# Up projections of a two-layer trunk: when products and operand sums are rounded, and when a group is convolved

## The chip, the cores and the metric

The kernel runs on one NeuronCore of a Trainium2 chip. The metric is the device time of one execution in microseconds (us), the median of several runs. The engines of the core work side by side and each takes its instructions in the order in which the program holds them: TensorE (PE) multiplies matrices, VectorE (DVE) and ScalarE (ACT) work element by element, GpSimd (POOL) and SyncE (SP) mostly issue DMAs. An instruction that reads what another engine made waits for that engine.

## The reference, cut to what matters

A trunk of two layers on 256 tokens of width 2048: a gated linear attention and a block-sparse attention, each followed by a gated FFN with a short convolution. Only the FFN matters here.

```python
def conv_ffn(x, norm_w, w_up, conv_w, conv_b, w_down):
    S = x.shape[1]
    h = rms_norm(x, norm_w) @ w_up                    # 256 x 2048 times 2048 x 11264
    hp = jnp.pad(h, ((0, 0), (CONV_WIDTH - 1, 0), (0, 0)))
    acc = conv_b
    for j in range(CONV_WIDTH):                       # width 3
        acc = acc + conv_w[j] * hp[:, j:j + S]
    a, u = jnp.split(acc, 2, axis=-1)
    return (jax.nn.silu(a) * u) @ w_down              # hidden 5632
```

## The kernel before, in words

**Precision and pieces.** All products are made in float32 accuracy from two rounded parts of each operand: a high part (`hi`) and the rest (`lo`), with three products hi·hi, hi·lo and lo·hi. Weights stream from HBM through SP into `wraw` tiles of 128 x 2048 (a chunk) and are split in pieces of 128 x 1024 at most: ACT rounds a piece to `whi` (L155), DVE subtracts to get `wlo` (L157). PE reads both. `step()` hands out one piece after the other; a "piece" is the unit in which the kernel counts time, and `after(n, job)` puts a job n pieces later.

**Blocks of seven products.** The up projection has 22 groups (J = 0 to 21) of 512 columns. Most are plain (L323, L326). Five pairs, the blocks that begin at J = 0, 4, 8, 12 and 16, are done together with fewer products: for chosen k a chunk yields seven products instead of eight (a "seven"). For a seven DVE makes sums of the weights (`t13` and `t24`, L116 to L118), and its four pieces are b11, wide, t13 and t24; DVE also makes sums of the activations (`comb`, in `combine`: L341 to L344), which are split like all operands (L482 on ACT, L483 on DVE). The order of k in a block is written out by hand in `ORDERS`; a `+` there marks a seven.

**From a group to the hidden operand.** A group's result is scaled, transposed into `z`, stored to DRAM and loaded back turned (`upT`, four DMAs on POOL). After `lag_of(J)` pieces `convolve` makes the taps of its first half (ACT L866, DVE L871 and L873), two pieces later those of the second half, then the product with silu (`product`: ACT L877, DVE L878), then `hidden`, which splits it to `hid` (L482 on ACT, L483 on DVE). The down projection reads `hid`. For J in `EARLY` = (1, 3, 5, 7, 9, 11, 13) `hidden` also starts the activation sums of the down projection's sevens: `combine` makes `comb` on DVE at once, and `rounded` splits it some pieces later.

**What sets the order.** The program is written piece by piece as above; then a scheduler of the tile framework fixes the order of each engine's instructions from its own estimates before the program runs. So a job that is moved by a piece also changes the order of its neighbours, on PE too.

Of the kernel before, what the change touches and what calls it, by code (L numbers as in the profile page):

```python
# [173 lines left out]
def trunk(ctx: ExitStack, tc: tile.TileContext, xT, x0g, x_tok, cst, msk, w1p, w2a, w_k, w_qa, w_v2, w_v, w_gs, w_g, w_go,  # L174
# [14 lines left out]
    def slot(shape, dt, name):  # L189
        return big.tile(shape, dt, name=name, tag="slot")  # L190

    def temp(name, shape=(128, 2, S), dt=F32):
        return tmp.tile(list(shape), dt, name=name, tag="temp")
# [81 lines left out]
    def col(c):  # L275
        return gn[:, c - C_GN:c - C_GN + 1] if C_GN <= c < C_GN + KT else cs[:, c:c + 1]
# [25 lines left out]
    def after(steps, job):  # L302
        later.append((cur[0] + steps, job))
# [10 lines left out]
    def gemm_tok(xs, groups=1, evacuate=lambda ps: ps):  # L314
        out_ = [accs() for _ in range(groups)]
        for q0 in range(0, KT, 2):
            for ps in out_:
                hi, lo = step()
                for ks in ((0,), (1,)) if cur[0] < 3 and groups > 1 else ((0, 1),):
                    tiles_ = [(q0 + k, t, k * 512) for k in ks for t in range(2)]  # L320
                    for x0 in (0, S):
                        for kt, t, c in tiles_:
                            T.matmul(ps[t], xs(kt)[:, x0 + 128 * t:x0 + 128 * t + 128], hi[:, c:c + 512],  # L323
                                     start=kt == 0 and x0 == 0, stop=False)
                    for kt, t, c in tiles_:
                        mm = T.matmul(ps[t], xs(kt)[:, 128 * t:128 * t + 128], lo[:, c:c + 512],  # L326
                                      start=False, stop=kt == KT - 1)
                newest[:] = [mm.ins]
        got = out_ if groups > 1 else evacuate(out_[0])
        ws.prefetch(cur[0])  # L330
        return got

    def behind(job):
        with ws.behind():
            job()

    def combine(k, halves_, into, wait=0):

        (a0, a1), (b0, b1) = halves_
        t = temp("comb", (128, 4, 128))  # L340
        V.tensor_add(t[:, 0], a1, b1)  # L341
        V.tensor_sub(t[:, 1], t[:, 0], a0)
        V.tensor_sub(t[:, 2], a0, a1)
        V.tensor_sub(t[:, 3], b0, t[:, 1])  # L344

        def rounded():
            c = slot([128, 4, 2, 128], F32R, "comb")
            split(c[:, :, 0], c[:, :, 1], t)
            into[k] = c

        if wait:
            after(wait, lambda: behind(rounded))
        else:
            rounded()
# [6 lines left out]
    def combine_late(k, xs, into, far=False):  # L361
        behind(lambda: combine_parts(k, xs, into, 5 if far else 2))
# [115 lines left out]
    def rows(xs):  # L478
        return lambda kt: xs[kt // 2][:, kt % 2, :]

    def split(dst_hi, dst_lo, src):
        A.copy(dst_hi, src)  # L482
        V.tensor_sub(dst_lo, src, dst_hi.bitcast(F32))  # L483
# [343 lines left out]
    def lag_of(J):  # L827

        if J + 1 in BLOCKS:
            order, n_tail = ORDERS["up"][BLOCKS.index(J + 1)]  # L830
            pairs = sum(seven for _, seven in order)
            return 2 * len(order) + 2 * pairs if pairs > 1 else 2 * (len(order) - n_tail) + 2 * pairs + 2
        if J - 1 in BLOCKS:
            return 13
        return 9 if J < FT // 2 - 2 else 7

    def ffn(layer, nrm, then):
        xs = rows(nrm.xs)
        hid, sums = [], {}
        cw = C_CW + layer * 3 * 2 * FT  # L840
        cb = C_CB + layer * 2 * FT
        turned = dram.tile([FT // 2, 16, 32, 4, 64], F32, name=f"turned{layer}")

        def square(ps):
            z = slot([128, 16, 2, 32], F32, "z")
            for t in range(2):
                tok = temp("tok", (128, 512))
                A.activation(tok, ps[t], AF.Copy, scale=nrm.woven[:, t:t + 1])
                V.transpose(z[:, :, t, :], tok.rearrange("p (a b) -> p a b", b=32))
            return z  # L850

        def store(J, z):
            nc.gpsimd.dma_start(turned[J].rearrange("(a i) r q c -> (i r) a (q c)", a=4),  # L853
                              z.rearrange("p (a q) t c -> p a (q t c)", a=4))

        def load(J):
            f = slot([128, 4, S], F32, "upT")
            for q in range(4):
                nc.gpsimd.dma_start(f[32 * q:32 * q + 32].rearrange("p a (i c) -> p (a i) c", i=4),  # L859
                                  turned[J][:, :, q, :].rearrange("a r c -> r a c"))  # L860
            return f

        def taps(j, t, au):
            for i in range(2):
                n = i * FT + j
                A.activation(au[i][:, j % 2, :], t[:, i, :], AF.Identity, bias=col(cb + n),  # L866
                             scale=col(cw + 2 * 2 * FT + n))
            for i in range(2):
                n = i * FT + j
                u = au[i][:, j % 2]  # L870
                V.scalar_tensor_tensor(u[:, 1:], t[:, i, :S - 1], col(cw + 2 * FT + n), u[:, 1:],  # L871
                                       op0=OP.mult, op1=OP.add)
                V.scalar_tensor_tensor(u[:, 2:], t[:, i, :S - 2], col(cw + n), u[:, 2:],  # L873
                                       op0=OP.mult, op1=OP.add)

        def product(au):
            A.activation(au[0], au[0], AF.Silu)  # L877
            V.tensor_mul(au[0], au[0], au[1])  # L878

        def hidden(J, au):  # L880
            hid.append(slot([128, 2, 2 * S], F32R, "hid"))
            split(hid[-1][:, :, :S], hid[-1][:, :, S:], au[0])
            if J in EARLY:
                combine(J, [(au[0][:, i, :128], au[0][:, i, 128:]) for i in range(2)], sums, 1)

        def convolve(J, t):
            au = temp("gate"), temp("value")
            behind(lambda: taps(2 * J, t[:, 0:2, :], au))
            after(2, lambda: behind(lambda: taps(2 * J + 1, t[:, 2:4, :], au)))
            after(3, lambda: behind(lambda: product(au)))  # L890
            after(4, lambda: behind(lambda: hidden(J, au)))

        f, first = {}, {}

        def onto(J, z):
            lag = lag_of(J)
            after(1, lambda: store(J, z))
            after(max(lag - 7, 2), lambda: f.update({J: load(J)}))
            after(lag, lambda: convolve(J, f[J]))

        def up_rows(t, J, x):
            if t == 0:
                first[J] = slot([128, 16, 2, 32], F32, "z")
            A.activation(x, x, AF.Copy, scale=nrm.woven[:, t:t + 1])
            V.transpose(first[J][:, :, t, :], x.rearrange("p (a b) -> p a b", b=32))  # L905
            if t:
                onto(J, first[J])

        x_sums = {}
        for J in range(FT // 2):  # L910
            if J == 2:
                after(1, lambda: combine_late(6, nrm.xs, x_sums))
            if J in BLOCKS:
                b = BLOCKS.index(J)
                down("up", nrm.xs, x_sums, None, lambda t, c, x: up_rows(t, J + c - 2 * b, x), {}, b)
            elif J in GROUPS:
                onto(J, gemm_tok(xs, 1, square))
        then(hid, sums)
# [380 lines left out]
```

## Time and profile before

| | us |
|---|---|
| median of 3 runs | 2144.72 |
| lowest and highest run | 2143.65, 2145.70 |
| profiled execution | 2145.70 |
| its span (first to last instruction) | 2143.9 |
| PE busy | 2135.4 |
| DVE busy | 1858.5 |
| ACT busy | 1346.8 |
| POOL busy | 290.1 |

The first conv-FFN's up projections lie between about 380 and 843 us of the span, the second's between about 1447 and 1913. "Busy" of PE means that a matmul was under way; the clock granted to it was 1.00 throughout. A row of the timeline gives the start, the duration, the engine, the line and what it writes and reads; a bracket at its end tells how long the engine was idle before it and what ended that. Consecutive instructions on DVE and ACT overlap a little, so what an instruction costs its queue is the distance from its start to the next start.

### The profile page before, as it was taken

How to read it: one execution, taken by the hardware profiler on the slowest of the kernel's cores; microseconds unless marked ns; L12 is line 12 of the kernel's file. 1: busy time of each engine (PE TensorE's matmuls, PEld its weight loads, DVE VectorE, ACT ScalarE, POOL GpSimd, SP SyncE). 2: the span in 40 equal slices, each digit the busy share in tenths (PEclk: the TensorE clock that was granted, in tenths of full speed). 3: DMA queues.
4: the chain of work that ended last, by engine and by line, in shares of the span. 5: the costliest groups of instructions: out<-in, count | busy, mean ns of one | idle time of the engine just before them, and what ended most of it. 6: DMA issues, size and time to landing. Idle time of an engine off the chain costs nothing.

```text
span 2143.9 us, 27139 instructions
## 1 busy us (share of the span) xinstructions
PE 2135.4 (100%) x9565; PEld 1767.7 (82%) x9565; DVE 1858.5 (87%) x2548; ACT 1346.8 (63%) x1881; POOL 290.1 (14%) x448
## 2 busy tenths in 40 slices
PE   9999999999999999999999999999999999999999
PEld 7888888888888888888888888888888878888887
DVE  6887788889999988998888789988899899879987
ACT  6657666566666666656566776555666666656554
POOL 1011111011021111000022341011110111210000
PEclk9999999999999999999999999999999999999999
DMA  8566677577687787575667986666776877775655
GB/s 323 182 222 212 215 243 275 203 241 252 219 266 252 236 265 248 205 255 217 226 252 258 285 283 210 227 244 209 240 256 218 260 249 236 262 248 207 245 205 168
DMA packets 90170, 510.11 MB, mean 238 GB/s; under 512 B 13569, under 2 KB 14609, under 8 KB 40114
## 3 DMA queue, kind: packets, MB, share of 16 engines
q1 hardware_dynamic: 60434, 417.31, 54.3%
q0 software_dynamic: 29024, 90.28, 15.4%
q8 instruction: 75, 1.23, 0.2%
q10 hardware_dynamic: 576, 0.79, 0.1%
q14 instruction: 61, 0.50, 0.1%
HBM read 463.22 MB, written 45.11 MB: 237 GB/s over the span
## 4 chain that ended last, share of the span: by engine, by line
PE 98%; DVE 1%; DMA 1%; issue 0%; ACT 0%; SPq 0%; ACTq 0%; DVEq 0%
PE p L404 55%; PE acc L323 27%; PE acc L326 13%; DVE wlo L157 1%; PE hf L941 0%; DMA wraw<-w_up1s 0%; PE sT L752 0%; PE o L769 0%; DMA wraw<-w_v 0%; PE s L1054 0%; ACT whi L155 0%; PE z L607 0%; PE o L555 0%; PE s L1052 0%; DVE t L116 0%
## 5 line engine op out<-in xcount | busy, mean ns | idle before, releaser
L155 ACT CAST whi<-wraw 128x1024 fp32r<-128x1024 f32 (+1 forms) x786 | 773.5, 1003 | 436.5 <-PE acc L323 212.1
L157 DVE TENSOR_TENSOR wlo<-wraw,whi 128x1024 fp32r<-128x1024 f32 (+1 forms) x786 | 899.9, 1160 | 165.2 <-ACT whi L155 141.2
L323 PE MATMUL acc<-whi,xw 128*128 128x512 f32 x2176 | 540.2, 389 | 0.7 <-ACT whi L155 0.6
L323 PEld LDWEIGHTS acc<-whi,xw 128*128 128x128 f32 x2176 | 407.6, 188 | 86.6 <-ACT whi L155 2.2
L404 PE MATMUL p<-whi,xw 128*128 128x512 f32 x1294 | 344.1, 389 | 0.0
L326 PE MATMUL acc<-wlo,xw 128*128 128x512 f32 x1088 | 291.9, 389 | 0.0
L404 PEld LDWEIGHTS p<-whi,xw 128*128 128x128 f32 x1294 | 242.8, 188 | 50.3 <-ACT whi L155 0.2
L404 PE MATMUL p<-whi,hid 128*128 128x512 f32 x1038 | 281.1, 389 | 0.0
L155 ACT CAST whi<-t 128x1024 fp32r<-128x1024 f32 x168 | 174.0, 1052 | 142.1 <-PE p L404 94.2
L326 PEld LDWEIGHTS acc<-wlo,xw 128*128 128x128 f32 x1088 | 204.1, 188 | 42.6 <-DVE wlo L157 0.3
L404 PEld LDWEIGHTS p<-whi,hid 128*128 128x128 f32 x1038 | 194.7, 188 | 40.3
L157 DVE TENSOR_TENSOR wlo<-t,whi 128x1024 fp32r<-128x1024 f32 x168 | 202.3, 1221 | 23.9 <-ACT whi L155 17.4
L404 PE MATMUL p<-whi,comb 128*128 128x512 f32 x672 | 218.8, 390 | 2.1 <-ACT whi L155 2.1
L404 PE MATMUL p<-wlo,xw 128*128 128x512 f32 x647 | 185.6, 390 | 0.0
L859 POOL DMA_DIRECT2D upT<-turned x176 | 114.1, 655 | 311.0 <-DVE wlo L157 82.4
L404 PEld LDWEIGHTS p<-whi,comb 128*128 128x128 f32 x672 | 126.1, 188 | 29.8 <-ACT whi L155 3.8
L404 PE MATMUL p<-wlo,hid 128*128 128x512 f32 x519 | 150.6, 389 | 0.0
L404 PEld LDWEIGHTS p<-wlo,xw 128*128 128x128 f32 x647 | 121.5, 188 | 25.0
L404 PE MATMUL p<-wlo,comb 128*128 128x512 f32 x336 | 115.6, 389 | 0.0
L404 PEld LDWEIGHTS p<-wlo,hid 128*128 128x128 f32 x519 | 97.4, 188 | 20.3
L116 DVE TENSOR_TENSOR t<-wraw 128x1024 f32<-128x1024 f32 x84 | 102.5, 1220 | 13.4 <-DMA wraw<-w_dn 6.0
L853 POOL DMA_DIRECT2D turned<-z x44 | 34.1, 775 | 502.5 <-DVE z L905 189.3
(257 smaller groups left out, 2259.8 us busy)
## 6 DMA issues: line engine op xcount, KB each, us to landing
wraw<-w_up SPq DMA_DIRECT2D x96, 1024.0 KB, 5.5
wraw<-w_dn SPq DMA_DIRECT2D x88, 1024.0 KB, 4.9
wraw<-w_up0s SPq DMA_DIRECT2D x40, 1024.0 KB, 5.7
wraw<-w_up1s SPq DMA_DIRECT2D x40, 1024.0 KB, 5.4
turned<-z POOLq DMA_DIRECT2D x44, 512.0 KB, 4.7
upT<-turned POOLq DMA_DIRECT2D x176, 128.0 KB, 5.4
wraw<-w_go SPq DMA_DIRECT2D x16, 1024.0 KB, 5.7
wraw<-w_kk SPq DMA_DIRECT2D x16, 1024.0 KB, 6.3
```

The costliest lines, as they stand in the source:

```text
L116: V.tensor_sub(t13, src[:, 512:1536], src[:, 0:1024])
L155: one = nc.scalar.copy(hi[:, a:b], src[:, a:b])
L157: two = nc.vector.tensor_sub(lo[:, a:b], src[:, a:b], hi[:, a:b].bitcast(F32))
L323: T.matmul(ps[t], xs(kt)[:, x0 + 128 * t:x0 + 128 * t + 128], hi[:, c:c + 512], start=kt == 0 and x0 == 0, stop=False)
L326: mm = T.matmul(ps[t], xs(kt)[:, 128 * t:128 * t + 128], lo[:, c:c + 512], start=False, stop=kt == KT - 1)
L404: mm = T.matmul(p[n], x[xi], w[wi][:, 512 * f:512 * f + 512], start=n not in begun, stop=left[n] == 0)
L853: nc.gpsimd.dma_start(turned[J].rearrange("(a i) r q c -> (i r) a (q c)", a=4), z.rearrange("p (a q) t c -> p a (q t c)", a=4))
L859: nc.gpsimd.dma_start(f[32 * q:32 * q + 32].rearrange("p a (i c) -> p (a i) c", i=4), turned[J][:, :, q, :].rearrange("a r c -> r a c"))
```

## The change

Three numbers. A block's second group (J = 1, 5, 9, 13, 17) is convolved 14 pieces after its products instead of 13, which also loads its `upT` one piece later. Every group's product is split to `hid` five pieces after its convolution began instead of four. And the activation sums of the groups in `EARLY` are rounded three pieces after that instead of one.

```diff
@@ lag_of @@
         if J - 1 in BLOCKS:
-            return 13
+            return 14
@@ hidden @@
             if J in EARLY:
-                combine(J, [(au[0][:, i, :128], au[0][:, i, 128:]) for i in range(2)], sums, 1)
+                combine(J, [(au[0][:, i, :128], au[0][:, i, 128:]) for i in range(2)], sums, 3)
@@ convolve @@
             after(3, lambda: behind(lambda: product(au)))
-            after(4, lambda: behind(lambda: hidden(J, au)))
+            after(5, lambda: behind(lambda: hidden(J, au)))
```

The order moves on PE, DVE and ACT; on POOL and SP it is the same. Three places follow, all in layer 0; the other blocks and layer 1 show the same pattern. Names carry buffer numbers.

ACT in block 4, around the split of the first t24 piece, `whi_4173`. Before (`gate_4053` belongs to J = 2, `gate_3952` and `comb_4064` to J = 1):

```order
L482 CAST hid_4061<-gate_3952 128x2x256
L482 CAST comb_4091<-comb_4064 128x4x128
L155 CAST whi_4094<-wraw_3964 128x1024
L866 ACTIVATE gate_4053<-upT_3894,cs_82 128x256
L866 ACTIVATE value_4054<-upT_3894,cs_82 128x256
L155 CAST whi_4118<-wraw_3986 128x512
L155 CAST whi_4136<-wraw_3986 128x1024
L155 CAST whi_4157<-t13_4070 128x1024
L877 ACTIVATE gate_4053<-gate_4053 128x512
L482 CAST hid_4154<-gate_4053 128x2x256
L155 CAST whi_4173<-t24_4071 128x1024
L155 CAST whi_4186<-wraw_4033 128x1024
```

Now (`gate_4051` is J = 2, `gate_3974` and `comb_4104` J = 1):

```order
L877 ACTIVATE gate_3974<-gate_3974 128x512
L155 CAST whi_4083<-wraw_3956 128x1024
L866 ACTIVATE gate_4051<-upT_3894,cs_82 128x256
L866 ACTIVATE value_4052<-upT_3894,cs_82 128x256
L155 CAST whi_4115<-wraw_3986 128x512
L482 CAST hid_4101<-gate_3974 128x2x256
L155 CAST whi_4133<-wraw_3986 128x1024
L155 CAST whi_4151<-t13_4062 128x1024
L877 ACTIVATE gate_4051<-gate_4051 128x512
L482 CAST hid_4167<-gate_4051 128x2x256
L482 CAST comb_4170<-comb_4104 128x4x128
L155 CAST whi_4173<-t24_4063 128x1024
```

The rounding of `comb` stood four splits ahead of `whi_4173` and stands directly before it now, behind `hid`.

DVE in the same place. Before:

```order
L157 TENSOR_TENSOR wlo_4137<-wraw_3986,whi_4136 128x1024
L157 TENSOR_TENSOR wlo_4158<-t13_4070,whi_4157 128x1024
L878 TENSOR_TENSOR gate_4053<-gate_4053,value_4054 128x512
L483 TENSOR_TENSOR hid_4154<-gate_4053,hid_4154 128x2x256
L157 TENSOR_TENSOR wlo_4174<-t24_4071,whi_4173 128x1024
L116 TENSOR_TENSOR t13_4181<-wraw_4098 128x1024
```

Now:

```order
L342 TENSOR_TENSOR comb_4104<-comb_4104,gate_3974 128x128
L157 TENSOR_TENSOR wlo_4152<-t13_4062,whi_4151 128x1024
L344 TENSOR_TENSOR comb_4104<-gate_3974,comb_4104 128x128
L878 TENSOR_TENSOR gate_4051<-gate_4051,value_4052 128x512
L483 TENSOR_TENSOR hid_4167<-gate_4051,hid_4167 128x2x256
L483 TENSOR_TENSOR comb_4170<-comb_4104,comb_4170 128x4x128
L157 TENSOR_TENSOR wlo_4174<-t24_4063,whi_4173 128x1024
```

Two of the activation sums (L342, L344) now stand ahead of the product L878, and the rest of `comb` (L483) ahead of `wlo_4174`.

DVE before block 8, where J = 5's second half is convolved (`gate_4691` before, `gate_4713` now). Before:

```order
L157 TENSOR_TENSOR wlo_4722<-wraw_4611,whi_4721 128x1024
L871 SCALAR_TENSOR_TENSOR gate_4691<-upT_4534,cs_82,gate_4691 128x255
L871 SCALAR_TENSOR_TENSOR value_4692<-upT_4534,cs_82,value_4692 128x255
L873 SCALAR_TENSOR_TENSOR gate_4691<-upT_4534,cs_82,gate_4691 128x254
L873 SCALAR_TENSOR_TENSOR value_4692<-upT_4534,cs_82,value_4692 128x254
L157 TENSOR_TENSOR wlo_4746<-wraw_4658,whi_4745 128x1024
L849 STREAM_TRANSPOSE z_4761<-tok_4762 128x16x32
```

Now:

```order
L157 TENSOR_TENSOR wlo_4722<-wraw_4611,whi_4721 128x1024
L157 TENSOR_TENSOR wlo_4740<-wraw_4658,whi_4739 128x1024
L849 STREAM_TRANSPOSE z_4755<-tok_4756 128x16x32
L849 STREAM_TRANSPOSE z_4755<-tok_4759 128x16x32
L157 TENSOR_TENSOR wlo_4763<-wraw_4658,whi_4762 128x1024
L871 SCALAR_TENSOR_TENSOR gate_4713<-upT_4547,cs_82,gate_4713 128x255
L116 TENSOR_TENSOR t13_4801<-wraw_4725 128x1024
L871 SCALAR_TENSOR_TENSOR value_4714<-upT_4547,cs_82,value_4714 128x255
L871 SCALAR_TENSOR_TENSOR gate_4790<-upT_4625,cs_82,gate_4790 128x255
L873 SCALAR_TENSOR_TENSOR gate_4713<-upT_4547,cs_82,gate_4713 128x254
```

The four taps of that half moved from between two plain pieces to behind two more splits, among the block's own work.

PE at the end of block 8's sevens. Before:

```order
L404 MATMUL p6_4953<-whi_5043,comb_3740 128x512
L404 MATMUL p4_4778<-whi_5043,xw_3328 128x512
L404 MATMUL p3_4777<-wlo_5017,comb_3740 128x512
L404 MATMUL p2_4776<-wlo_5017,xw_3328 128x512
L404 MATMUL p2_4776<-whi_5050,xw_3338 128x512 x4
L404 MATMUL p5_4941<-wlo_5034,comb_3740 128x512
L404 MATMUL p7_4942<-wlo_5034,comb_3740 128x512
```

Now:

```order
L404 MATMUL p3_4775<-wlo_5017,comb_3740 128x512
L404 MATMUL p2_4774<-wlo_5017,xw_3328 128x512
L404 MATMUL p5_4941<-wlo_5034,comb_3740 128x512
L404 MATMUL p7_4942<-wlo_5034,comb_3740 128x512
L404 MATMUL p6_4953<-whi_5043,comb_3740 128x512
L404 MATMUL p4_4776<-whi_5043,xw_3328 128x512
L404 MATMUL p6_4953<-whi_5043,comb_3740 128x512
L404 MATMUL p4_4776<-whi_5043,xw_3328 128x512
L404 MATMUL p2_4774<-whi_5050,xw_3338 128x512 x4
```

The two matmuls on `wlo_5034` stood behind the four on `whi_5043` and four on `whi_5050`, and stand ahead of those eight now.

## Rows read from the trace of the kernel before

**Rows 1.** The page: busy time, and the chain that ended last

```profile
PE 2135.4 (100%) x9565; PEld 1767.7 (82%) x9565; DVE 1858.5 (87%) x2548; ACT 1346.8 (63%) x1881; POOL 290.1 (14%) x448
...
PE 98%; DVE 1%; DMA 1%; issue 0%; ACT 0%; SPq 0%; ACTq 0%; DVEq 0%
```

**Rows 2.** The chain in order of time: start us, us, what

```profile
98.81 40.80 PE p L404 x180
```

**Rows 3.** PE's waits: who waited for whom: us in total, times, longest

```profile
PE p L404 <- ACT whi L155: 2.1, 3, 1.3
```

**Rows 4.** Windows: busy us (and count) of PE, PEld, DVE, ACT, POOL; clock, DMA

```profile
477.00:491.00 14.00, 14.00 (x63) 11.47 (x62) 13.02 (x15) 8.25 (x10) 0.00 (x0) 1.00 0.46 166
543.00:581.00 38.00, 38.00 (x169) 31.45 (x169) 38.00 (x53) 26.05 (x35) 3.37 (x5) 1.00 0.69 230
...
1712.00:1731.00 19.00, 17.15 (x75) 13.46 (x74) 18.03 (x23) 10.87 (x14) 2.59 (x4) 1.00 0.68 218
```

**Rows 5.** Timeline of ACT, block 4, layer 0: start us, us, instruction

```profile
477.19 0.62 ACT L482 CAST hid<-gate 128x512 fp32r<-128x512 f32 x1 [2.41 <-DVE gate L878]
477.72 1.04 ACT L155 CAST whi<-t 128x1024 fp32r<-128x1024 f32 x1
...
488.75 1.05 ACT L155 CAST whi<-t 128x1024 fp32r<-128x1024 f32 x1 [4.61 <-DVE t L118]
```

**Rows 6.** Timeline of PE at the end of that stretch

```profile
489.90 0.45 PE L404 MATMUL p<-whi,comb 128*128 128x512 f32 x1
```

**Rows 7.** Timeline of DVE in the same stretch

```profile
478.79 1.22 DVE L157 TENSOR_TENSOR wlo<-t,whi 128x1024 fp32r<-128x1024 f32 x1 [0.26 <-ACT whi L155]
479.94 1.22 DVE L116 TENSOR_TENSOR t<-wraw 128x1024 f32<-128x1024 f32 x1
...
487.95 0.68 DVE L118 TENSOR_TENSOR t<-wraw,t 128x512 f32<-128x512 f32 x1
...
489.27 0.69 DVE L118 TENSOR_TENSOR t<-wraw,t 128x512 f32<-128x512 f32 x1
```

**Rows 8.** Timeline of DVE, block 12, layer 0: an activation sum and the next start

```profile
638.47 0.28 DVE L344 TENSOR_TENSOR comb<-gate,comb 128x128 f32<-128x128 f32 x1
638.67 0.69 DVE L117 TENSOR_TENSOR t<-t,wraw 128x512 f32<-128x512 f32 x1
```

**Rows 9.** Timeline of ACT there: the rounding of `comb` and the next start

```profile
638.78 0.63 ACT L482 CAST comb<-comb 128x512 fp32r<-128x512 f32 x1 [4.22 <-DVE comb L344]
639.31 1.04 ACT L155 CAST whi<-wraw 128x1024 fp32r<-128x1024 f32 x1
```

**Rows 10.** Timeline of ACT, block 12, layer 1

```profile
1702.48 0.60 ACT L866 ACTIVATE gate<-upT,cs 128x256 f32<-128x256 f32 x1 [3.27 <-DMA upT<-turned]
...
1717.30 1.04 ACT L155 CAST whi<-t 128x1024 fp32r<-128x1024 f32 x1
```

**Rows 11.** Timeline of PE, block 12, layer 1: its two waits

```profile
1718.40 0.50 PE L404 MATMUL p<-whi,comb 128*128 128x512 f32 x1 [1.33 <-ACT whi L155]
...
1729.43 0.50 PE L404 MATMUL p<-whi,comb 128*128 128x512 f32 x1 [0.52 <-ACT whi L155]
```

**Rows 12.** Timeline of ACT and of PE, block 12, layer 0

```profile
658.47 1.05 ACT L155 CAST whi<-t 128x1024 fp32r<-128x1024 f32 x1 [4.22 <-DVE t L118]
...
660.02 0.39 PE L404 MATMUL p<-whi,comb 128*128 128x512 f32 x1
```

**Rows 13.** Timeline of DVE before block 8, layer 0: the first tap of four

```profile
542.76 1.23 DVE L157 TENSOR_TENSOR wlo<-wraw,whi 128x1024 fp32r<-128x1024 f32 x1 [1.45 <-ACT whi L155]
543.90 0.48 DVE L871 SCALAR_TENSOR_TENSOR gate<-upT,cs,gate 128x255 f32<-128x255 f32 x1
...
545.48 1.23 DVE L157 TENSOR_TENSOR wlo<-wraw,whi 128x1024 fp32r<-128x1024 f32 x1
```

**Rows 14.** Timeline of DVE, end of block 8's sevens: `wlo_5034` and the next

```profile
577.23 2.36 DVE L157 TENSOR_TENSOR wlo<-t,whi 128x1024 fp32r<-128x1024 f32 x2
```

**Rows 15.** Timeline of PE there: `wlo_5034` twice, then `wlo_5044`

```profile
581.14 0.84 PE L404 MATMUL p<-wlo,comb 128*128 128x512 f32 x3
```

## Prediction

> **What bounds the kernel now.** I read the page first, then PE's waits, then the windows of the two conv-FFN layers, and last the timelines of ACT, DVE and PE in the tightest windows. The page shows PE busy for 2135.4 of 2143.9 us, and PE carries 98% of the chain that ended last [rows 1]. A matmul of 512 columns takes its turn every 40.80 / 180 = 0.227 us [rows 2]. PE is idle for 8.5 us in all, so no change of order can gain more than that. PE's waits name the weight split: 2.1 us in three waits for ACT's `whi` [rows 3].
>
> The bound lies on PE, but with thin cover in places. Each weight piece of 128x1024 is rounded by ACT (`whi`, L155), its rest is made by DVE (`wlo`, L157), and PE reads both. In a block, a chunk of seven products has DVE make sums (L116 to L118) as well. `wlo` and L116 take 1.22 us, L118 on half the width 0.68 [rows 7]; a chunk has one `wlo` of half and three of full width, one L116 and two half sums: 4 x 1.22 + 3 x 0.68 = 6.9 us (of each some 0.08 lies beside the next), while PE's 21 matmuls last 21 x 0.227 = 4.8 us. So DVE falls behind in every row of sevens and PE lives off the lead. The windows show it: DVE 38.00 of 38.00 us busy between 543 and 581, 13.02 of 14.00 between 477 and 491 [rows 4]. What counts is the spare: how long a piece was ready before PE took it.
>
> **The places.** Blocks start at J = 4, 8, 12 and 16; J = 1, 5, 9, 13 are the second groups of the blocks before. The change delays the convolution of those by one piece, which puts their last steps into the next block's row of sevens, in two layers: eight places.
>
> **Blocks 4 and 12 (type A).** In block 4, ACT rounds `hid` at 477.19 and the t24 piece right behind it at 477.72; the same ACT row of splits then ends, after a wait of 4.61 us for DVE's t24 sum, at 488.75 + 1.05 = 489.80 [rows 5]. PE takes that piece at 489.90 [rows 6]: spare 0.10 us. From `wlo` at 478.79 to L118 at 489.27 DVE shows no idle time [rows 7]. What is added ahead of this stretch therefore reaches PE whole. By the order, three things now stand there: on DVE L342 and L344 of J = 1's operand sums, ahead of the product L878 for which `hid` waits (0.20 us each: L344 to the next start is 638.47 to 638.67 [rows 8]), and on ACT the rounding `comb` between `hid` and `whi`, 0.53 us (638.78 to 639.31 [rows 9]). Together 0.93 us. DVE's own `comb` rest (L483) stands beside ACT's split and is hidden by the wait for `whi`. Before, all of it was done ahead of these rows.
>
> [...] The rounding of `comb` feeds nothing before the down projection; if ACT let the ready `whi` pass it, its 0.53 us would cost nothing. In the trace `whi` starts at 477.72, straight behind a `hid` that had waited 2.41 us [rows 5]. [...]
>
> A PE start follows its split by 0.06 us where PE waits for it (1717.30 + 1.04 = 1718.34 to 1718.40 [rows 10, 11]), so each place loses 0.93 - spare + 0.06:
> - J = 4, both layers: spare 0.10, loss 0.89 each (I take layer 1 as layer 0), 1.78.
> - J = 12, layer 0: 658.47 + 1.05 = 659.52 against PE at 660.02 [rows 12], spare 0.50, loss 0.49 at the least. If the four taps of type B also slip behind DVE's last idle time here, 1.58 more. Between 0.49 and 2.07 I take 1.25, about the middle, since the order of this block interleaves those taps with the splits.
> - J = 12, layer 1: PE already waits there, 1.33 and 0.52 us [rows 11], so there is no spare: 0.5 more than in layer 0, 1.75 (bounds 0.99 and 2.57).
>
> **Blocks 8 and 16 (type B).** DVE's last idle time is 1.45 us ahead of `wlo` at 542.76; behind it stand the four taps of J = 5's second half, 543.90 to 545.48, 1.58 us, and then DVE is full through 581 [rows 4, 13]. In the new order these taps come one piece later, after the `wlo` for which DVE idles again. The idle time is now wasted and 1.58 us of work is pushed into the full stretch. PE's order changes as well: the `wlo_5034` matmuls come 8 matmuls earlier, 8 x 0.227 = 1.81 us. That `wlo` ended at 577.23 + 1.22 = 578.45 [rows 14], and PE took it at 581.14 [rows 15]: spare 2.69. Loss: 1.58 + 1.81 - 2.69 + 0.06 = 0.76 us. Bounds: 0 if PE's new order costs nothing by itself (1.58 is less than 2.69), 1.64 if the spare is used up elsewhere. The value 0.76 follows the order as it stands. Four times: 3.04.
>
> **What costs nothing.** POOL and SP issue the same DMAs in the same order. Work on every engine is the same in amount. The later `hid` and `comb` of the last groups are read only in the down projection, hundreds of microseconds on; only J = 19 to 21 are close, and the down projection reads them in its tail. The rounding of J = 3, 7 and 11 also moves two pieces, within stretches that are already in the account.
>
> **Sum.** 1.78 + 1.25 + 1.75 + 3.04 = 7.82, say 7.8 us. The profiled execution took 2145.7 us (span 2143.9 and 1.8 around it), so it would be 2153.5. It lies 1.0 above the median of the runs, 2144.7; the median after is forecast at 2152.5. A measurement of this kernel can tell about 0.2% (4.3 us) from no change.
>
> **The rivals.**
> - *Absorbed.* The sums and roundings leave their old places, and DVE starts the row of sevens with more lead, so that spares grow by what is moved. For it: total work is unchanged, and PE waits only 8.5 us in the whole span [rows 1]. Against it: the lead is limited by three split buffers, so a lead cannot be stored beyond them, and the windows are full [rows 4]. Time: 0 to 3 us more, 2146.
> - *The stall in layer 1 goes.* In block 12 of layer 1 ACT waited 3.27 us for J = 10's `upT` to land [rows 10], and PE lost 1.85 us behind it [rows 11]. If delaying J = 9's convolution lets the splits go ahead of that wait, this comes back, provided type A and B stay under their spares: 2144.7 - 1.85 = 2142.9. It decides if ACT's splits stand ahead of the late taps. Against it: J = 10's own lag is unchanged, and J = 9's work lands in the same window. It is faster than 0.2% only if over half of the other idle time went too.
> - *The stall grows.* The late `upT` and J = 9's work add up in block 12 of layer 1, and a second late landing does the same elsewhere: one or two more waits of about 3.3 us [rows 10], 2156 to 2159. For it: landings differ between executions; against it: the runs of before differ by 2 us only.
>
> **How the numbers follow.** Forecast (eight stalls, 2149 to 2156): 0.70. Stall grows: 0.12. Absorbed: 0.13. Stall goes: 0.05. Slower by over 0.2% means above 2149.0: forecast and grown stall, 0.82. Within: absorbed and most of the fourth, 0.15. Faster: 0.03. The low ends of all terms add up to 1.78 + 0.49 + 0.99 + 0 = 3.3 us (2148.0), the high ends to 1.78 + 2.07 + 2.57 + 4 x 1.64 = 13.0 (2157.7). The range takes both in, 2147.5 to 2158.
>
> **What would show it.** Right: PE's waits for ACT `whi` and DVE `wlo` total 8 to 11 us instead of 2.1, in pairs at 479/490, 651/662 and singly near 580 and 752, and again in layer 1; DVE idle behind `wlo` at about 545; ACT's `comb` directly behind `hid` in block 4. Wrong: PE without idle time at 480 to 491, or the loss in one place only (a DMA), or idle time at the start of the down projections.

## The result, and the profile after

| | before | changed |
|---|---|---|
| median of 6 runs, us | 2144.69 | 2156.72 |
| lowest to highest, us | 2142.53 to 2147.68 | 2152.52 to 2159.87 |
| profiled execution, us | 2145.70 | 2159.07 |
| its span, us | 2143.9 | 2157.3 |

The changed kernel is slower: ratio 1.0055, 95% interval 1.0041 to 1.0069, that is 12.0 us between the medians. The forecast was 2152.5 us with 2147.5 to 2158 as its range.

The page of the changed kernel answers [rows 1]:

```profile
span 2157.3 us, 27122 instructions
...
PE 2142.9 (99%) x9565; PEld 1765.6 (82%) x9565; DVE 1858.0 (86%) x2548; ACT 1345.0 (62%) x1881; POOL 290.0 (13%) x448
```

The counts of instructions are the same on every engine shown, and the busy time of DVE, ACT and POOL is the same within 2 us; the 13.4 us that the span grew are waiting. PE's waits answer [rows 3]:

```profile
PE p L404 <- DVE wlo L157: 5.0, 9, 0.9
PE p L404 <- ACT whi L155: 3.5, 10, 0.5
```

Three waits have become nineteen. They add up to 8.5 us, but cost more than that. Each matmul is shown busy for 0.39 us although the next one starts 0.23 us after it, so 0.16 us of a wait passes as work of the matmul before it (at 581.81: 0.39 busy, 0.89 idle, next start 583.09); and, as the rows below show, the second matmul after a wait starts late as well. What a wait costs is therefore read from start to start: the distance between two starts less 0.227. Over the whole profile these excesses add up to 7.4 us before and 19.8 after, 12.4 more.

The windows answer [rows 4] (same columns):

```profile
477.00:491.00 14.00, 13.60 (x59) 10.54 (x57) 13.10 (x17) 7.53 (x10) 0.00 (x0) 1.00 0.39 141
543.00:581.00 38.00, 37.54 (x163) 29.86 (x162) 34.86 (x51) 23.06 (x31) 3.37 (x5) 1.00 0.64 216
```

In the first window PE did 59 matmuls instead of 63. In the second DVE was busy for 34.86 of 38 us, where before it was full: 3.1 us of its time are lost there, and PE did six matmuls fewer. The granted clock is 1.00 in both.

**Block 4 (type A).** The timeline of ACT in the changed kernel, beside [rows 5]:

```profile
477.91 0.62 ACT L482 CAST hid<-gate 128x512 fp32r<-128x512 f32 x1 [1.84 <-DVE gate L878]
478.44 0.61 ACT L482 CAST comb<-comb 128x512 fp32r<-128x512 f32 x1
478.96 1.04 ACT L155 CAST whi<-t 128x1024 fp32r<-128x1024 f32 x1
...
489.99 1.05 ACT L155 CAST whi<-t 128x1024 fp32r<-128x1024 f32 x1 [5.31 <-DVE t L118]
```

`comb` stands between `hid` and the t24 piece's `whi`, which starts 1.24 us later than before (478.96 against 477.72). Of these, 0.27 us are older than the block: the matmul that started at 470.19 before starts at 470.45 here. The other 0.97 are the block's own, against the forecast's 0.93. DVE in the same place:

```profile
476.99 0.29 DVE L344 TENSOR_TENSOR comb<-gate,comb 128x128 f32<-128x128 f32 x1
477.19 0.69 DVE L878 TENSOR_TENSOR gate<-gate,value 128x512 f32<-128x512 f32 x1
478.56 0.69 DVE L483 TENSOR_TENSOR hid<-gate,hid 128x512 fp32r<-128x512 f32 x1 [0.69 <-ACT hid L482]
479.17 0.68 DVE L483 TENSOR_TENSOR comb<-comb 128x512 fp32r<-128x512 f32 x1
480.03 1.23 DVE L157 TENSOR_TENSOR wlo<-t,whi 128x1024 fp32r<-128x1024 f32 x1 [0.18 <-ACT whi L155]
```

The t24 piece's `wlo` starts at 480.03 instead of 478.79 [rows 7], again 1.24 later. The two sums (L342 stands a little earlier, ahead of a `wlo`) stand ahead of L878 and DVE's part of `comb` is hidden, as forecast. PE then, beside [rows 6]:

```profile
480.05 0.50 PE L404 MATMUL p<-whi,comb 128*128 128x512 f32 x1
480.39 0.39 PE L404 MATMUL p<-whi,xw 128*128 128x512 f32 x1
...
491.09 0.50 PE L404 MATMUL p<-whi,comb 128*128 128x512 f32 x1 [0.49 <-ACT whi L155]
491.43 0.40 PE L404 MATMUL p<-whi,xw 128*128 128x512 f32 x1
```

PE loses time in two steps, 480 and 491, as the forecast's pair says. From start to start the four type A places lose 0.95, 0.95, 1.08 and 0.98 us (blocks 4 and 12 of layer 0, then of layer 1), 4.0 in all.

**Block 8 (type B).** DVE ahead of it in the changed kernel, beside [rows 13]:

```profile
546.71 1.22 DVE L157 TENSOR_TENSOR wlo<-wraw,whi 128x1024 fp32r<-128x1024 f32 x1 [1.46 <-ACT whi L155]
...
550.18 0.47 DVE L871 SCALAR_TENSOR_TENSOR gate<-upT,cs,gate 128x255 f32<-128x255 f32 x1
552.34 1.22 DVE L116 TENSOR_TENSOR t<-wraw 128x1024 f32<-128x1024 f32 x1 [1.68 <-DMA wraw<-w_up0s]
553.49 0.48 DVE L871 SCALAR_TENSOR_TENSOR value<-upT,cs,value 128x255 f32<-128x255 f32 x1
```

The idle time of 1.46 us between two `wlo` is there, and the taps have moved behind it, as forecast. What the forecast does not have is a second idle time: L116, the sum for the next seven, waits 1.68 us for a weight chunk, and the remaining taps stand in DVE's queue behind it. The kernel before, where the taps and L878 still stand ahead of that L116, has no wait there:

```profile
550.74 1.22 DVE L116 TENSOR_TENSOR t<-wraw 128x1024 f32<-128x1024 f32 x1
```

PE at the end of the block in the changed kernel, beside [rows 15]:

```profile
573.27 1.19 PE L404 MATMUL p<-wlo,xw 128*128 128x512 f32 x4 [0.28 <-DVE wlo L157]
...
576.69 0.50 PE L404 MATMUL p<-whi,comb 128*128 128x512 f32 x1 [0.18 <-ACT whi L155]
577.03 0.39 PE L404 MATMUL p<-whi,xw 128*128 128x512 f32 x1
...
583.09 0.73 PE L404 MATMUL p<-wlo,comb 128*128 128x512 f32 x2 [0.89 <-DVE wlo L157]
```

Instead of one wait there are three, and the four type B places lose 2.48, 2.86, 2.44 and 2.73 us, 10.5 in all. The same wait of L116 stands at all four. DVE's rows there, in order of time (blocks 16 of layer 0, 8 and 16 of layer 1):

```profile
726.50 1.23 DVE L116 TENSOR_TENSOR t<-wraw 128x1024 f32<-128x1024 f32 x1 [2.08 <-DMA wraw<-w_up0s]
1627.30 1.23 DVE L116 TENSOR_TENSOR t<-wraw 128x1024 f32<-128x1024 f32 x1 [1.62 <-DMA wraw<-w_up1s]
1801.38 1.23 DVE L116 TENSOR_TENSOR t<-wraw 128x1024 f32<-128x1024 f32 x1 [1.97 <-DMA wraw<-w_up1s]
```

Before, L116 waited for no chunk at these places. With DVE's 1.46 us, the 1.68 make up the 3.14 us that the window above lacks. The forecast's 0.76 us and the wait of L116 add up to about the loss of a place:

| place | wait of L116 | + 0.76 | measured on PE |
|---|---|---|---|
| block 8, layer 0 | 1.68 | 2.44 | 2.48 |
| block 16, layer 0 | 2.08 | 2.84 | 2.86 |
| block 8, layer 1 | 1.62 | 2.38 | 2.44 |
| block 16, layer 1 | 1.97 | 2.73 | 2.73 |

That the sums agree to a few hundredths is in part chance: in experiment 6, without the wait, a place loses about 1.0 us by the same rule, so a wait of L116 costs PE some 0.2 us less than its length.

The account of the profile: 4.0 + 10.5 = 14.5 lost, less some 2.4 for the stall of block 12 in layer 1 [rows 11], which this execution does not have: 12.1 of the 12.4 us.

### The profile page after: what moved, and what is told of

Its sections match the earlier page's. It is cut to its first block, busy times and chain, and to the rows that moved or that the text cites. A ratio compares the mean times of both kernels' runs of the same rounds, so it can differ in the third digit from the quotient of the medians.

```text
span 2157.3 us, 27122 instructions
## 1 busy us (share of the span) xinstructions
PE 2142.9 (99%) x9565; PEld 1765.6 (82%) x9565; DVE 1858.0 (86%) x2548; ACT 1345.0 (62%) x1881; POOL 290.0 (13%) x448
## 5 line engine op out<-in xcount | busy, mean ns | idle before, releaser
L404 PE MATMUL p<-whi,xw 128*128 128x512 f32 x1294 | 343.9, 390 | 0.0
L404 PEld LDWEIGHTS p<-whi,xw 128*128 128x128 f32 x1294 | 242.6, 188 | 50.5 <-ACT whi L155 0.7
L404 PE MATMUL p<-whi,hid 128*128 128x512 f32 x1038 | 281.1, 389 | 0.0
L404 PEld LDWEIGHTS p<-whi,hid 128*128 128x128 f32 x1038 | 194.7, 188 | 40.4
L404 PE MATMUL p<-whi,comb 128*128 128x512 f32 x672 | 220.9, 393 | 3.7 <-ACT whi L155 3.5
L404 PE MATMUL p<-wlo,xw 128*128 128x512 f32 x647 | 186.8, 390 | 1.2 <-DVE wlo L157 1.2
L404 PEld LDWEIGHTS p<-whi,comb 128*128 128x128 f32 x672 | 125.8, 188 | 37.6 <-ACT whi L155 12.2
L404 PE MATMUL p<-wlo,hid 128*128 128x512 f32 x519 | 150.6, 389 | 0.0
L404 PEld LDWEIGHTS p<-wlo,xw 128*128 128x128 f32 x647 | 121.1, 188 | 27.6 <-DVE wlo L157 2.9
L404 PE MATMUL p<-wlo,comb 128*128 128x512 f32 x336 | 116.8, 391 | 3.8 <-DVE wlo L157 3.8
L116 DVE TENSOR_TENSOR t<-wraw 128x1024 f32<-128x1024 f32 x84 | 102.4, 1219 | 20.4 <-DMA wraw<-w_go 5.8
L404 PEld LDWEIGHTS p<-wlo,hid 128*128 128x128 f32 x519 | 97.4, 188 | 20.2
```

What stands on the lines that cost most here:

```text
L116: V.tensor_sub(t13, src[:, 512:1536], src[:, 0:1024])
L404: mm = T.matmul(p[n], x[xi], w[wi][:, 512 * f:512 * f + 512], start=n not in begun, stop=left[n] == 0)
```

## The experiments

Two questions stood open: whether the roundings or the later convolution cause the loss (theories ROUNDING and LAG), and what makes type B three times as large as forecast: the taps that slip behind DVE's idle time (TAPS) or the chunk that lands late beside the loads of `upT` (DMA). Experiments 1 to 4 ran beside 23 runs of the kernel before (median 2144.41), 5 to 7 on another chip beside 28 (2145.32). A ratio is to the kernel before of the same set; medians of different sets, the changed kernel's 2156.72 among them, compare only roughly. What a place loses is read from start to start throughout.

**1. The later convolution alone (lag_only), on the kernel before.**

```diff
         if J - 1 in BLOCKS:
-            return 13
+            return 14
```

> The kernel before with one number changed: a block's second group is convolved 14 pieces after its products instead of 13; hidden stays at 4, the rounding of the sums at 1. Theory LAG (the later convolution alone pushes taps, product and split into the next block's row of sevens; the roundings hardly matter): 10 to 13 us over the kernel before, PE waits near 480/491, 564 to 583, 653/664, 737 to 757 and again in layer 1. Theory ROUNDING (as the prediction's working has it, the rounding of comb between hid and whi makes type A, some 4 us, and the lag makes type B, some 10 us as measured after): about 8 to 10 us over, PE waits at 564 to 583 and 737 to 757, but under 0.3 us in all at 480 and 491.

Measured: 2160.34 us, ratio 1.0066 (1.0054 to 1.0079). By the medians that is 15.9 us, more than either theory expected. The lag alone gives the whole loss, if not more than that (the interval of the change, 1.0041 to 1.0069, overlaps). The profiled execution took 2156.31 us, 4.0 under the median, so its rows account for part of the loss only. PE's waits in it are nearly all for `whi`:

```profile
PE p L404 <- ACT whi L155: 9.4, 10, 2.2
```

Type A loses there without any rounding on ACT between `hid` and `whi`. ACT in block 4 of this kernel:

```profile
473.82 0.62 ACT L482 CAST comb<-comb 128x512 fp32r<-128x512 f32 x1
475.41 0.64 ACT L877 ACTIVATE gate<-gate 128x512 f32<-128x512 f32 x1 [0.97 <-DVE gate L873]
478.08 0.62 ACT L482 CAST hid<-gate 128x512 fp32r<-128x512 f32 x1 [2.04 <-DVE gate L878]
478.61 1.05 ACT L155 CAST whi<-t 128x1024 fp32r<-128x1024 f32 x1
```

There `comb` is rounded ahead of the silu, and `whi` stands straight behind `hid`. DVE in the same place:

```profile
476.76 0.69 DVE L483 TENSOR_TENSOR comb<-comb 128x512 fp32r<-128x512 f32 x1
477.36 0.69 DVE L878 TENSOR_TENSOR gate<-gate,value 128x512 f32<-128x512 f32 x1
```

The other half of `comb` (L483, 0.60 to the next start) stands on DVE ahead of L878, for which `hid` and so `whi` wait. The sums get in the way on the one engine or on the other. Type B shows another stall, on ACT and then on PE:

```profile
562.47 0.62 ACT L482 CAST comb<-comb 128x512 fp32r<-128x512 f32 x1 [1.65 <-DVE comb L344]
564.08 0.50 PE L404 MATMUL p<-whi,comb 128*128 128x512 f32 x1 [0.97 <-ACT whi L155]
```

ACT's `comb` waited for L344 with `whi` behind it, and PE waited for that `whi`. The changed kernel, with later roundings, does not have this stall, but three others in its place. So the time of the loss is the lag's, but type B is not the same loss in the two kernels: here it is 6.2 us over the four places and has a late chunk (1.08 us of L116's waiting) in one of them only.

**2. The roundings alone (hid_comb_only), on the kernel before.**

```diff
-                combine(J, [... for i in range(2)], sums, 1)
+                combine(J, [... for i in range(2)], sums, 3)
-            after(4, lambda: behind(lambda: hidden(J, au)))
+            after(5, lambda: behind(lambda: hidden(J, au)))
```

> The other two numbers alone: hidden at 5 pieces and the rounding of the sums at 3, the lag left at 13. Theory LAG: within 2 us of the kernel before, no PE waits near 480 to 491 and 564 to 583. Theory ROUNDING: some 4 us over the kernel before, with PE waits of 0.7 to 1.0 us at about 480 to 491 and 652 to 664 in layer 0 and the same in layer 1.

Measured: 2145.93 us, ratio 1.0010 (1.0001 to 1.0019). That is within the 2 us of LAG. PE has no wait in the blocks of layer 0. What its profile has is one stall in block 4 of layer 1 (1.14 and 0.65 us); there `comb` and `hid` waited on ACT for L344 and L878, and what made these late was not followed. By themselves the roundings cost 1.5 us by the medians, 4.1 at the upper end of the interval; ROUNDING falls as the cause of the whole loss.

**3. The sums rounded much later (comb_late), on the changed kernel.**

```diff
-                combine(J, [... for i in range(2)], sums, 3)
+                combine(J, [... for i in range(2)], sums, 16)
```

> The changed kernel, but the sums of the EARLY groups are rounded 16 pieces after hidden instead of 3, behind the row of sevens. Theory LAG: 1 to 2 us less than the changed kernel, since 0.53 us of ACT and 0.60 us of DVE leave each of eight places, but the taps still lie there: about 2155. Theory ROUNDING: type A shrinks to 0.40 us less the spare, 2 to 4 us less than the changed kernel, 2152 to 2154, with under 0.5 us of PE waits at 480 to 491.

Measured: 2153.99 us, ratio 1.0044 (1.0032 to 1.0056), 2.7 us under the changed kernel by the medians, with intervals that overlap. Here ROUNDING's numbers are met and not LAG's: the time is just within its 2152 to 2154, and PE waits 0.24 us at 490.61, under its 0.5. ACT in block 4, and PE's wait:

```profile
477.95 0.62 ACT L482 CAST hid<-gate 128x512 fp32r<-128x512 f32 x1 [1.84 <-DVE gate L878]
478.47 1.05 ACT L155 CAST whi<-t 128x1024 fp32r<-128x1024 f32 x1
...
490.61 0.50 PE L404 MATMUL p<-whi,comb 128*128 128x512 f32 x1 [0.24 <-ACT whi L155]
```

With `comb` gone from between them, `whi` starts 0.52 us behind `hid` instead of 1.05, and block 4 loses 0.51 us instead of 0.95. So in block 4 of the changed kernel the 0.53 us of the rounding count nearly in full (0.44), as the forecast had it. Block 12 gains less (0.84 instead of 0.95 in layer 0). So the roundings cost nothing in layer 0 without the lag, and something with it. The larger part of what this profile gains is not type A (4.0 to 2.7 us over its four places) but type B (10.5 to 6.3): in blocks 8 the order on DVE is that of the changed kernel, but L116 waits no more and PE loses 1.03 and 1.02 us; in both blocks 16 L116 still waits (0.8 and 1.2 us).

**4. A piece earlier instead of later (lag_12), on the kernel before:** `return 12`.

> The kernel before with the second group's convolution one piece earlier, 12 instead of 13, nothing else. Theory LAG: the taps leave the row of sevens by one more piece, the spare at 490 grows from 0.1 us to some 0.5 to 1 us; time as the kernel before or up to 3 us less, since before lost only 2 us in such places in its profiled run. Rival (any shift from 13 hurts, since 13 was where taps fall into idle time of DVE): 3 to 8 us over the kernel before.

Measured: 2147.67 us, ratio 1.0010 (1.0001 to 1.0020). By the ratio that is 2.1 us over the kernel before, by the medians 3.3: not the gain that LAG allowed, and the rival's 3 to 8 is not clearly met either. PE's waits move to the plain groups (1.3 us at 795.7 and 1.8 at 1695.6). They stand behind ACT's taps, which now come before their `upT` has landed:

```profile
793.60 0.60 ACT L866 ACTIVATE gate<-upT,cs 128x256 f32<-128x256 f32 x1 [6.27 <-DMA upT<-turned]
1693.02 0.60 ACT L866 ACTIVATE gate<-upT,cs 128x256 f32<-128x256 f32 x1 [7.12 <-DMA upT<-turned]
```

The kernel before is not beaten by going the other way.

**5. The second half's taps put back (half2_back), on the changed kernel.** For the second groups of blocks they follow the first half by one piece instead of two.

```diff
-            after(2, lambda: behind(lambda: taps(2 * J + 1, t[:, 2:4, :], au)))
+            after(1 + (J - 1 not in BLOCKS), lambda: behind(lambda: taps(2 * J + 1, t[:, 2:4, :], au)))
```

> The changed kernel, but in a block's second group (J = 1, 5, 9, 13, 17) the taps of the second half come one piece after those of the first instead of two, so these four taps stand where they stood in the kernel before; all else stays late. Theory TAPS (1.58 us of taps pushed behind DVE's last idle time is the core of the loss at blocks 8 and 16, and makes room at 4 and 12): 1 to 4 us over the kernel before, 8 to 11 less than the changed kernel; at 546 to 585 PE loses under 1.3 us instead of 2.4. Rival (the late product, hid and comb of those groups do it, the taps little): within 3 us of the changed kernel, 2154 to 2158.

Measured: 2150.62 us, ratio 1.0026 (1.0012 to 1.0039), half of the loss. In time neither theory is met: 5.3 us over the kernel before instead of 1 to 4, some 6 under the changed kernel instead of 8 to 11 or under 3. The profiled execution (2148.62) lies 2.0 under the median. What decides for TAPS is the place. The order of the block's end goes back as well, with both parts of the forecast's term. The window shows it:

```profile
543.00:581.00 38.00, 38.00 (x170) 31.45 (x169) 38.00 (x55) 26.18 (x35) 3.37 (x5) 1.00 0.66 218
```

DVE and PE are full again, without a wait in block 8 of layer 0, and L116 does not wait there. TAPS holds there: with the taps' place, type B goes from 10.5 to 1.0 us in the profile. About 0.6 us of type A stays in three of its places (0.47 to 0.52, and 0.11 for the late second matmul), against 0.95 to 1.08, so these taps had a part in type A as well. Block 12 of layer 1 loses 0.97 and 0.68 us in its two steps. In block 16 of layer 1 L116 still waits 1.1 us and PE loses the 1.0 us that is left.

**6. and 7. Without the loads beside the chunk (less_load, and less_load_before as its control).** The groups J = 2, 6, 10, 14 and 18 do not load their own `upT`; they are convolved with that of the group before them, so the hidden values of these groups are others. The same edit is made in the changed kernel and in the kernel before.

```diff
-            after(max(lag - 7, 2), lambda: f.update({J: load(J)}))
+            after(max(lag - 7, 2), lambda: f.update({J: load(J) if J - 2 not in BLOCKS else f[J - 1]}))
```

> The changed kernel without the load of upT for the groups J = 2, 6, 10, 14, 18, which take the previous group's upT instead (that part of the computation is left out); the order on PE and ACT is as in the changed kernel, on DVE nearly. In the changed kernel DVE waits 1.6 to 2.1 us in L116 at 552, 726, 1627, 1801 for a weight chunk that lands 7.0 us after its issue. Theory DMA (those loads, issued at about 536, crowd the chunk): the chunk lands 1.5 us or more earlier, the L116 waits at the four places fall under 0.5 us each, PE's losses there fall from 2.3 to 2.9 us to some 1 us; 5 to 7 us less than the changed kernel. Rival ISSUE (the chunk is late because its buffer comes free late): the waits in L116 stay over 1.2 us, time within 2 us of the changed kernel.

> Control: the kernel before with the same loads left out (J = 2, 6, 10, 14, 18 take the previous group's upT; that part of the computation is left out). Both theories: within 2 us of the kernel before, since PE lost nothing in layer 0's blocks there.

Measured: 2152.44 us, ratio 1.0031 (1.0021 to 1.0041), and for the control 2146.11 us, 1.0003 (0.9993 to 1.0013). Leaving the loads out takes the ratio from 1.0055 to 1.0031 in the changed kernel (the intervals just touch), 4.3 us by the medians and some 5 by the ratios, where 5 to 7 was expected. In the kernel before it changes nothing. DVE of less_load ahead of block 8:

```profile
547.23 1.23 DVE L157 TENSOR_TENSOR wlo<-wraw,whi 128x1024 fp32r<-128x1024 f32 x1 [1.46 <-ACT whi L155]
...
551.09 1.22 DVE L116 TENSOR_TENSOR t<-wraw 128x1024 f32<-128x1024 f32 x1
552.23 0.48 DVE L871 SCALAR_TENSOR_TENSOR value<-upT,cs,value 128x255 f32<-128x255 f32 x1
```

The order and the idle time of 1.46 us are those of the changed kernel, but L116 does not wait. The end of that block, DVE and then PE:

```profile
580.55 1.24 DVE L157 TENSOR_TENSOR wlo<-t,whi 128x1024 fp32r<-128x1024 f32 x1
...
580.85 0.39 PE L404 MATMUL p<-wlo,xw 128*128 128x512 f32 x1
581.84 0.73 PE L404 MATMUL p<-wlo,comb 128*128 128x512 f32 x2 [0.60 <-DVE wlo L157]
```

PE loses 581.84 - 580.85 - 0.23 = 0.76 us in this wait: the forecast's term. The forecast's parts can be read as well. This `wlo` (`wlo_5034` of the kernel before) ends at 581.79 instead of 578.45, 3.34 us later; 1.75 of these are older than the block (the matmul of 545.10 starts at 546.85), and the other 1.59 match the forecast's 1.58 of taps. The other three places show 0.76, 0.76 and 0.96 in the wait, the last with 0.21 of waiting in L116. With the late matmuls around the waits the places lose 0.98, 0.98, 0.97 and 1.14, 4.1 in all instead of 10.5. DMA holds too: the chunk's late landing is the rest of type B. The chunk that L116 reads took 7.03 us in the changed kernel (545.28 to 552.32), 4.85 here (545.80 to 550.65). It was issued later here and still came in time, so the rival ISSUE is out.

What delays the chunk can be followed on POOL, where the loads start some 0.7 us after the store ahead of them has landed. In the changed kernel:

```profile
527.84 0.77 POOL L853 DMA_DIRECT2D turned<-z  x1 [0.85 <-DVE gate L871]
535.74 2.59 POOL L859 DMA_DIRECT2D upT<-turned  x4 [7.12 <-PE acc L326]
```

(The bracket names PE, but the loads follow the landing of the store by 0.69 us here, 0.74 before and 0.68 in lag_only.) The store took 7.21 us to land, at 535.05, and the four loads behind it were issued from 535.74 and took 9.2 to 9.6 each. The chunk issued at 539.86 beside them took 9.61 and the next 7.03. Before, the store took 5.48, the loads began at 534.18 and took 7.6 to 8.5, the chunk issued at 539.17 took 7.73 and the next 5.36. In lag_only (loads from 534.36, 6.0 to 6.3 each, next chunk 4.77) and comb_late (6.4 to 7.2, next chunk 4.74) the same chunk came in time. What L116's chunk meets is in part the loads and in part the chunk ahead of it: in the changed kernel it was issued at 545.28, while the loads were under way until 546.97 and the chunk before it until 549.47; in lag_only it was issued at 544.89, when the loads had landed (542.57) and the chunk before it was about to (544.96). The delay is older than the store, too: the four loads ahead of it took 7.5 to 7.9 us, before 5.0 to 5.2. So it is the moment at which loads and chunks meet; which of the three edits sets it was not told apart.

## Why the prediction was right, and where its sum was off

**The side, and the places.** Slower, at the eight places named, by the order of ACT and DVE around the sevens: all of that is in the trace. The rival "absorbed" is out, since PE loses time at all eight.

**Type A.** Forecast 0.89 and 0.89 (block 4 in either layer), 1.25 and 1.75 (block 12); measured 0.95, 1.08, 0.95 and 0.98. The size 0.93 - spare + 0.06 held in block 4, to 0.06 and 0.19 us. In block 12 of layer 0, with the spare of 0.50 that was read there, it gives 0.49, and the middle of the bounds gave 1.25; the 0.95 lies between, and half2_back (0.63) puts some 0.3 of it down to the taps, not 1.58. For layer 1 the term counted on no spare because PE waited there before [rows 11], behind a late landing of `upT` [rows 10]. The changed kernel has no such wait: the term was 0.77 too high, and 2.4 us of the profile before went as well. Here the rival "the stall goes" was right for this one place. The late landing comes back in other kernels, lag_only and half2_back,

```profile
1709.53 0.60 ACT L866 ACTIVATE gate<-upT,cs 128x256 f32<-128x256 f32 x1 [2.72 <-DMA upT<-turned]
1703.18 0.60 ACT L866 ACTIVATE gate<-upT,cs 128x256 f32<-128x256 f32 x1 [2.30 <-DMA upT<-turned]
```

and PE loses 2.24 and 0.68, and 0.97 and 0.68 us behind it. With one profile of each kernel it cannot be told whether it belongs to the kernel or to the execution.

The naming of causes was incomplete: that the rounding `comb` stands on ACT between `hid` and `whi` is worth 0.44 us in block 4 of the changed kernel, but lag_only loses as much there without it. What the two kernels share is that J = 1's work comes a piece later; that this costs the same in whatever order is argued from these two and not shown.

The forecast counted the rounding's 0.53 us whole, which holds only if ACT does not let `whi` pass it. In block 4 the trace shows that: `whi` starts behind the rounding (478.44 to 478.96), though the t24 sum that it reads was done at 473.21 (L118, 472.52 + 0.69), and in comb_late, with no rounding there, it starts 0.53 us nearer to `hid`. For the other places it was not shown.

**Type B: the term that was mis-sized.** Forecast 0.76 a place, 3.04 in all, bounds 0 to 1.64; measured 2.44 to 2.86, 10.5 in all. The working itself (1.58 us of taps, 1.81 us of PE order, a spare of 2.69) was right: less_load measures 0.76 in the wait and 1.59 for the taps. What it left out there is the late matmuls behind a wait, some 0.2 us a place. The step that failed is "POOL and SP issue the same DMAs in the same order", put down under what costs nothing. The order is the same, but the times are not: a chunk landed later, L116 waited 1.6 to 2.1 us for it on a DVE that had lost its lead, and the taps behind it waited too: in block 8 of layer 0 the `value` of J = 5 had come from ACT by 549.76 (L866, 549.17 + 0.59), but its first tap on DVE started at 553.49, behind L116. The upper bound left room for a spare used up elsewhere, but not for a new wait ahead of the full stretch.

**The sum.** 7.8 forecast, 12.0 measured between the medians. In the profile: type B 7.5 more than forecast, type A 0.8 less, the stall of layer 1 2.4 gone. The forecast's 8 to 11 us of PE waits came out as 8.5, but by luck: for the reason given above waits understate the loss, 14.5. That the range held the time is luck in part, too. Its upper end was the sum of all upper bounds; all four type B places went beyond theirs (1.64), and block 12, which stayed far below its own (0.95 of 2.07, 0.98 of 2.57), and the stall that went made up for it. 2156.7 is outside the 2149 to 2156 that the forecast gave to its eight stalls, and inside the 2156 to 2159 of "the stall grows". That rival had the right kind of cause, a late landing, but looked for it in `upT` and in one block, not in the weight chunks of four.

## What to carry to other kernels

A job moved by a single piece can cost what it pushes into the next stretch where the engine has no idle time left; find the last idle time ahead of that stretch and see which side of it the job falls on (here 1.58 us of taps behind DVE's last idle time made a `wlo` 1.59 us later in less_load, and PE lost 0.76 us waiting for it). An unchanged order of DMAs is not unchanged timing (here 7.03 us to land instead of 5.36 for the chunk that L116 reads): beside every idle time that is moved or shortened, look at how late the transfers land that the next instruction in the queue needs, and give the sum a term for it. And a stall that starts from a late landing may come and go with small changes (block 12 of layer 1: there in three of the profiles above, where ACT waited 2.3 to 3.3 us for `upT`, gone in the changed kernel): count it neither as lasting nor as gone until a second profile shows it.

## What the runs showed of the hardware that was not expected

- After a wait of PE the second matmul also comes late: 0.34 us from start to start instead of 0.227 (576.69 to 577.03, 491.09 to 491.43; behind the waits between matmuls of L404 in all nine profiles it is 0.108 to 0.115 us late). With the 0.16 us hidden in the busy time of the matmul before it, a wait costs about 0.27 us more than its row says.
- A weight chunk of 1 MB took 4.84 and 4.85 us to land without the loads of `upT` or another chunk beside it (issued at 540.37 and 545.80 in less_load). In the changed kernel it took 9.61 us beside the loads and 4.0 us of the chunk before it, and the next one 7.03, beside the end of the loads and 4.2 us of the chunk before it.
